# Feed-forward up product as seven block products, gated products in DRAM, and a down product with tokens stationary

## Chip, cores and metric

One core of a Trainium2 chip (trn2) runs the whole program. The metric is the device time of one execution in microseconds; the kernel before takes 2195.97 us, the median of 3 runs (2193.7 to 2197.01).

## What is computed

One inference step of a one-layer decoder over 1024 prompt tokens and 8 sample tokens (NT = 1032 columns). Attention, gated linear attention and cross attention come first and are not touched. The change is in what follows them:

```python
    u, g = jnp.split(h @ w_up, 2, axis=-1)
    g_ext = jnp.concatenate([conv_past.astype(g.dtype), g], axis=1)
    gc = conv_b + sum(conv_w[j] * g_ext[:, j:j + t] for j in range(CONV_W))
    out = (jax.nn.gelu(gc) * u) @ w_down
...
    x1 = x + merged @ p['w_o']
    ffn, conv_state = _conv_ffn(_rmsnorm(x1, p['g_ffn']), conv_past, p['w_up'], p['conv_w'], p['conv_b'], p['w_down'])
    y = x1 + ffn
```

`w_up` is 1024 x 5632 (u and g), `w_down` 2816 x 1024. The 2816 feed-forward columns are cut into 22 tiles f of 128. Everything is fp32 outside; a product is done as three fp32r matmuls, high part by high part, high by low and low by high, after each operand x is split into hi = round(x) and lo = x - hi.

## The kernel before, in words

**Merge and x1 (lines 1541 to 1578).** For each block i of 128 tokens (0 to 7, then the 8 sample tokens as block 8) the product with `w_o` runs with tokens stationary and 512 output columns moving (line 1563), 48 matmuls a block. DVE adds the result to x, SP stores the row block to `d_x1`, and `norm_rows` (ACT square, POOL power, DVE scale) gives the normed rows. One half block later `norm_turn` (line 261) turns them with 8 PE transposes and splits them by `split` (line 198: ACT writes hi, DVE writes lo) into `f_hi` and `f_lo`, 128 x 8 x 1032 each, which keep the names m_hi and m_lo in the trace.

**Up product (lines 1609 to 1644).** Per f, `dense` (line 218) is called twice, for g and for u. It loads a 128 x 8 x 128 slice of `w_up` into a `wraw` tile (three slots), splits it into `whi` and `wlo` (two slots each), and runs `mm3` (line 211) on three chunks of tokens, 384, 384 and 264 wide: 8 k by 3 = 24 matmuls a chunk, 72 a product. Chunk sums go alternately to the PSUM names bd and bt (`bank_f`). The g sums are copied by ACT into `gx_`; POOL and DVE do the convolution, ACT the gelu (lines 1627 to 1630); the u sums are multiplied on DVE and split again into `a_hi` and `a_lo`.

**Down product (lines 1602 to 1607).** After each group of three f (two in the last two groups) `down` multiplies the group's gated tiles by `w_down`, weights stationary, tokens moving, and `devac` adds each sum into `yacc`, which lies with output columns on the partitions. So at the end `y_half` (line 1673) turns `yacc` back with PE transposes, adds `x1` and stores. The last group's product and these turns are interleaved (lines 1684 to 1697).

**What sets the order.** The Tile framework takes the instructions of all engines in the order of the code as priorities and moves one forward when its inputs are there. A tile of a pool has a name and a number of slots of that name (`bufs`); a new tile waits until an older one of the same name is given back, which for a stored tile is when its DMA has landed. All the DMAs here are issued by SP, in one queue.

Of the kernel before, what the change touches and what calls it, by code (L numbers as in the profile page):

```python
# [17 lines left out]
P = 128  # L18
D = 1024
# [104 lines left out]
def body(ctx, tc, A):  # L124
# [16 lines left out]
    def bank_t():  # L141
        return pt.tile([P, 512], FT, name="bt")
# [1386 lines left out]
    with pool("fs", side="right") as fs, pool("wo") as wo:  # L1529
# [9 lines left out]
        scn = fs.tile([16, FF], FT, name="scn")  # L1539
        SY.dma_start(scn, A["state_conv"].rearrange("b t f -> (b t) f"))  # L1540
        prev = None
        mst = wo.tile([P, 8, 40], FR, name="mst")
        V.memset(mst.bitcast(FT), 0.0)
        V.tensor_copy(mst[:, :, 0:8], m_hi[:, :, S:])
        V.tensor_copy(mst[:, :, 32:40], m_lo[:, :, S:])
        for i in range(9):
            k = P if i < 8 else NB
            ts = slice(i * P, i * P + k)
            xt = wo.tile([P, D], FT, name="x2", bufs=3)
# [1 line left out]
            for hf in range(2):  # L1551
                cs = slice(hf * 512, (hf + 1) * 512)
                b = bank_s()
                if i == 8:
                    for j in range(8):
                        for w_ in range(2):
                            PE.matmul(b[:40], mst[:, j], owt[j][w_][:, cs], start=j + w_ == 0, stop=j + w_ == 8)
                    V.tensor_tensor(xt[:k, cs], xt[:k, cs], b[32:40], op=OP.add)
                else:
                    n = 0  # L1560
                    for j in range(8):
                        for a_, w_ in ((m_hi, 0), (m_lo, 0), (m_hi, 1)):
# [21 lines left out]
    sizes = (3, 3, 3, 3, 3, 3, 2, 2)
    groups = [list(range(sum(sizes[:g]), sum(sizes[:g + 1]))) for g in range(len(sizes))]
    assert groups[-1][-1] == FT_N - 1
    yacc = fp.tile([P, 8, NT], FT, name="yacc")
    GW = 2 + S + 24
    fh = lambda k: f_hi[:, k]
    fl = lambda k: f_lo[:, k]  # L1590
    ups = {}

    def devac(gi, m, c, cs, b):
        if gi == 0:
            SC.activation(yacc[:, m, cs], b, AF.Copy)
# [3 lines left out]
    def w_dn(gi):
        return A["w_down"].rearrange("(f p) m -> p f m", p=P)[:, groups[gi][0]:groups[gi][-1] + 1]  # L1600

    def down(gi):
        ats = ups.pop(gi)
        for m in range(8):
            dense(len(ats), lambda raw: SY.dma_start(raw, w_dn(gi)[:, :, m * P:(m + 1) * P]),
                  lambda k: ats[k][0], lambda k: ats[k][1],
                  lambda c, cs, b: devac(gi, m, c, cs, b), bank=bank_s)

    for gi, grp in enumerate(groups):
        ats = ups[gi] = []  # L1610
        for f in grp:
            gx_ = fp.tile([P, GW], FT, name="gx_", bufs=2)
            V.memset(gx_[:, 0:2], 0.0)
            dv = gx_[:, 2 + S:].rearrange("p (b x) -> p b x", x=3)
            V.tensor_copy(dv[:, :, 0:2], scT[:, f].rearrange("p (b t) -> p b t", t=2))

            def gevac(c, cs, b, gx_=gx_, dv=dv):
                n = b.shape[-1] - (NB if c == 2 else 0)
                SC.activation(gx_[:, 2 + cs.start:2 + cs.start + n], b[:, :n], AF.Copy)
                if c == 2:  # L1620
                    V.tensor_copy(dv[:, :, 2], b[:, n:])
            dense(8, colfill(A["w_up"], FF + f * P), fh, fl, gevac, bank=bank_f)
            V.tensor_copy(gl[f // 12][:, 0:2, f % 12], gx_[:, S:S + 2])
            V.tensor_copy(gl[f // 12][:, 2:10, f % 12], dv[:, :, 2])
            cv = fp.tile([P, GW], FT, name="cv", bufs=2)
            n = GW - 2
            G.tensor_scalar(cv[:, :n], gx_[:, :n], cwt[:, 0, f:f + 1], cwt[:, 3, f:f + 1], op0=OP.mult, op1=OP.add)
            V.scalar_tensor_tensor(cv[:, :n], gx_[:, 1:n + 1], cwt[:, 1, f:f + 1], cv[:, :n], op0=OP.mult, op1=OP.add)
            V.scalar_tensor_tensor(cv[:, :n], gx_[:, 2:n + 2], cwt[:, 2, f:f + 1], cv[:, :n], op0=OP.mult, op1=OP.add)
            SC.activation(cv[:, :n], cv[:, :n], AF.Gelu_apprx_tanh)  # L1630
            a_hi = fp.tile([P, NT], FR, name="a_hi", bufs=5)
            a_lo = fp.tile([P, NT], FR, name="a_lo", bufs=5)
            cvd = cv[:, 2 + S:2 + S + 24].rearrange("p (b x) -> p b x", x=3)[:, :, 0]

            def uevac(c, cs, b, cv=cv, cvd=cvd, a_hi=a_hi, a_lo=a_lo):
                w = b.shape[-1]
                n = w - (NB if c == 2 else 0)
                t = fp.tile([P, CW], FT, name="au", bufs=2)
                V.tensor_tensor(t[:, :n], cv[:, cs.start:cs.start + n], b[:, :n], op=OP.mult)
                if c == 2:  # L1640
                    V.tensor_tensor(t[:, n:w], cvd, b[:, n:], op=OP.mult)
                split(a_hi[:, cs], a_lo[:, cs], t[:, :w])
            dense(8, colfill(A["w_up"], f * P), fh, fl, uevac, bank=bank_f)
            ats.append((a_hi, a_lo))
            if gi and f == grp[0]:
                down(gi - 1)

    wl = []
    for k in range(2):
        raw = wp.tile([P, 1024], FT, name="wraw", bufs=3)  # L1650
        hi = wp.tile([P, 1024], FR, name="whi", bufs=2)
        lo = wp.tile([P, 1024], FR, name="wlo", bufs=2)
        SY.dma_start(raw, w_dn(gi)[:, k])
        split(hi, lo, raw)
        wl.append((hi, lo))
    x_3 = fp.tile([P, 3, D], FT, name="x_3")
    for i in range(3):
        SY.dma_start(x_3[:, i], d_x1[i * P:(i + 1) * P])
    xl = fq.tile([P, 8, NT], FR, name="m_hi").bitcast(FT)
    for i in range(3, 8):  # L1660
        SY.dma_start(xl[:, i, :D], d_x1[i * P:(i + 1) * P])
    SY.dma_start(xl[:NB, 0, :D], d_x1[S:])
    for x in range(2):
        f0, n = (0, 12) if x == 0 else (12, 10)
        b = bank_t()
        tr(b[:10 * n, :P], gl[x].rearrange("p t f -> p (t f)"))
        go_ = fp.tile([P, P], FT, name="go_", bufs=2)
        V.tensor_copy(go_[:10 * n], b[:10 * n, :P])
        for dst, r0, t in ((A["conv_p"].rearrange("b t (f p) -> (b t) f p", p=P), 0, 2),
                           (A["conv_s"][:, 1].rearrange("b (f p) -> b f p", p=P), 2 * n, 8)):  # L1670
            SY.dma_start(dst[:, f0:f0 + n], go_[r0:r0 + t * n])

    def y_half(i, hf):
        k = P if i < 8 else NB
        cs = slice(hf * 512, (hf + 1) * 512)
        xt = x_3[:, i, cs] if i < 3 else xl[:, i % 8, cs]
        b = bank_t()
        for a in range(4):
            tr(b[:k, a * P:(a + 1) * P], yacc[:, 4 * hf + a, i * P:i * P + k])
        V.tensor_tensor(xt[:k], xt[:k], b[:k], op=OP.add)  # L1680
        dst = A["y_p"].rearrange("b (i p) d -> (b i) p d", p=P)[i] if i < 8 else A["y_s"].rearrange("b t d -> (b t) d")
        SY.dma_start(dst[:, cs], xt[:k])

    for c, (c0, c1) in enumerate(CHS):
        cs = slice(c0, c1)
        for m in range(8):
            ms = slice(m * P, (m + 1) * P)
            b = bank_s()[:, :c1 - c0]
            n = 0
            for k in range(2):  # L1690
                for w_, a_ in ((0, 0), (0, 1), (1, 0)):
                    PE.matmul(b, wl[k][w_][:, ms], ats[k][a_][:, cs], start=n == 0, stop=n == 5)  # L1692
                    n += 1
            devac(gi, m, c, cs, b)
            if m % 4 == 3:
                for i in ((0, 1, 2), (3, 4, 5), (6, 7, 8))[c]:
                    y_half(i, m // 4)
# [35 lines left out]
```

## Time and profile before

| | |
|---|---|
| Median of 3 runs | 2195.97 us |
| The profiled execution's own time | 2186.02 us |
| Its span on the chip | 2184.2 us |
| PE busy | 98% of the span |
| DVE, ACT, POOL busy | 48%, 33%, 14% |
| Feed-forward part, 1420.86 us to the end | 763.3 us |

Times in rows are microseconds from the start of the span unless ns is written. PE is the matmul engine, PEld its weight load, SPq the queue that issues DMAs. A matmul row's own duration includes its passage through the pipeline; how often the next one starts is the rate.

### The profile page before, as it was taken

How to read it: one execution, taken by the hardware profiler on the slowest of the kernel's cores; microseconds unless marked ns; L12 is line 12 of the kernel's file. 1: busy time of each engine (PE TensorE's matmuls, PEld its weight loads, DVE VectorE, ACT ScalarE, POOL GpSimd, SP SyncE). 2: the span in 40 equal slices, each digit the busy share in tenths (PEclk: the TensorE clock that was granted, in tenths of full speed). 3: DMA queues.
4: the chain of work that ended last, by engine and by line, in shares of the span. 5: the costliest groups of instructions: out<-in, count | busy, mean ns of one | idle time of the engine just before them, and what ended most of it. 6: DMA issues, size and time to landing. Idle time of an engine off the chain costs nothing.

```text
span 2184.2 us, 35331 instructions
## 1 busy us (share of the span) xinstructions
PE 2138.6 (98%) x13964; PEld 1938.9 (89%) x13964; DVE 1051.5 (48%) x2618; ACT 714.8 (33%) x1545; POOL 301.2 (14%) x401
## 2 busy tenths in 40 slices
PE   7999899999999899999999999999999999999999
PEld 6999888888998798866667997799999999999998
DVE  5224455455533845288775475333243434344455
ACT  5323233333433522386653132222322121212120
POOL 3003400000100420075441310000000000000000
PEclk9999999999999999999999999999999999999999
DMA  6242633453264335631102555120211112120113
GB/s 182 97 109 85 240 110 127 174 174 117 75 213 136 102 90 147 128 89 42 39 9 90 165 165 178 68 63 26 62 36 56 51 41 59 30 67 25 59 54 129
DMA packets 241343, 213.48 MB, mean 98 GB/s; under 512 B 48614, under 2 KB 215386, under 8 KB 239626
## 3 DMA queue, kind: packets, MB, share of 16 engines
q1 hardware_dynamic: 240602, 194.45, 29.9%
q0 software_dynamic: 576, 16.78, 1.9%
q8 instruction: 110, 1.80, 0.3%
q14 instruction: 55, 0.45, 0.1%
HBM read 162.55 MB, written 48.73 MB: 97 GB/s over the span
## 4 chain that ended last, share of the span: by engine, by line
PE 86%; DMA 3%; issue 3%; DVE 2%; POOL 2%; ACT 1%; SPq 0%; POOLq 0%; ACTq 0%; DVEq 0%
PE bd L215 19%; PE bd L343 15%; PE bt L215 15%; PE bs L215 10%; PE bt L167 7%; PE bo L892 3%; PE bs L1563 3%; PE bs L765 2%; DMA Gt<-in_cache_kv,idx 2%; PE bs L591 1%; PE bd L765 1%; POOL rr L195 1%; PE bs L1692 1%; PE bs L474 1%; PE bo L1205 1%
## 5 line engine op out<-in xcount | busy, mean ns | idle before, releaser
L200 DVE TENSOR_TENSOR wlo<-wraw,whi 128x1024 fp32r<-128x1024 f32 (+3 forms) x183 | 173.0, 946 | 384.9 <-ACT whi L199 383.1
L343 PE MATMUL bd<-h_hi,whi 128*128 128x384 f32 (+1 forms) x960 | 322.1, 335 | 2.2 <-ACT st L334 2.2
L343 PE MATMUL bd<-h_lo,whi 128*128 128x384 f32 (+1 forms) x960 | 313.0, 326 | 0.0
L343 PE MATMUL bd<-h_hi,wlo 128*128 128x384 f32 (+1 forms) x960 | 312.1, 325 | 0.0
L199 ACT ACTIVATE whi<-wraw 128x1024 fp32r<-128x1024 f32 (+3 forms) x185 | 154.8, 838 | 404.1 <-PE bs L215 165.6
L343 PEld LDWEIGHTS bd<-h_hi,whi 128*128 128x128 f32 x960 | 182.0, 190 | 12.5 <-issue 8.1
L215 PE MATMUL bd<-m_lo,whi 128*128 128x384 f32 (+1 forms) x624 | 190.8, 319 | 0.0
L215 PE MATMUL bt<-m_lo,whi 128*128 128x384 f32 (+1 forms) x624 | 190.7, 319 | 0.0
L343 PEld LDWEIGHTS bd<-h_lo,whi 128*128 128x128 f32 x960 | 182.4, 190 | 3.5 <-issue 2.9
L343 PEld LDWEIGHTS bd<-h_hi,wlo 128*128 128x128 f32 x960 | 181.9, 189 | 3.1 <-issue 2.6
L215 PE MATMUL bd<-m_hi,wlo 128*128 128x384 f32 (+1 forms) x528 | 168.9, 320 | 0.0
L215 PE MATMUL bt<-m_hi,wlo 128*128 128x384 f32 (+1 forms) x528 | 168.8, 320 | 0.0
L215 PE MATMUL bd<-m_hi,whi 128*128 128x384 f32 (+1 forms) x528 | 168.7, 319 | 0.0
L215 PE MATMUL bt<-m_hi,whi 128*128 128x384 f32 (+1 forms) x528 | 168.6, 319 | 0.0
L215 PE MATMUL bs<-a_hi,wlo 128*128 128x384 f32 (+1 forms) x480 | 153.6, 320 | 0.0
L215 PE MATMUL bs<-a_lo,whi 128*128 128x384 f32 (+1 forms) x480 | 153.4, 320 | 0.0
L215 PE MATMUL bs<-a_hi,whi 128*128 128x384 f32 (+1 forms) x480 | 153.4, 320 | 0.0
L195 POOL TENSOR_TENSOR rr<-rv,cb 128x1 f32<-128x1 f32 (+7 forms) x46 | 52.3, 1138 | 649.7 <-DVE rv L194 622.5
L1597 DVE TENSOR_TENSOR yacc<-yacc,bs 128x384 f32<-128x384 f32 (+1 forms) x168 | 85.7, 512 | 89.8 <-PE bs L215 84.1
L215 PEld LDWEIGHTS bd<-m_lo,whi 128*128 128x128 f32 x624 | 115.9, 188 | 0.0
L215 PEld LDWEIGHTS bt<-m_lo,whi 128*128 128x128 f32 x624 | 115.9, 188 | 0.0
L215 PEld LDWEIGHTS bd<-m_hi,whi 128*128 128x128 f32 x528 | 99.1, 188 | 0.1
(810 smaller groups left out, 4513.3 us busy)
## 6 DMA issues: line engine op xcount, KB each, us to landing
wraw<-in_w_in SPq DMA_DIRECT2D x46, 512.0 KB
wraw<-in_w_up SPq DMA_DIRECT2D x44, 512.0 KB
tg<-d_g SPq DMA_DIRECT2D x24, 516.0 KB
d_g<-st SPq DMA_DIRECT2D x48, 192.0 KB
wraw<-in_w_down SPq DMA_DIRECT2D x48, 192.0 KB
d_z<-st SPq DMA_DIRECT2D x32, 192.0 KB
of<-d_o SPq DMA_DIRECT2D x12, 512.0 KB
xt<-in_x_prompt SPq DMA_DIRECT2D x8, 512.0 KB
```

What stands on the lines that cost most here:

```text
L167: PE.transpose(out, in_, ident[:k, :k])
L195: G.tensor_tensor(r[:k], v[:k], C("mhalf")[:k, :n], op=OP.pow)
L199: SC.activation(hi, src, AF.Copy)
L200: eng.tensor_tensor(lo, src, hi.bitcast(FT), op=OP.subtract)
L215: PE.matmul(out, a[:, k], b(k), start=n == 0, stop=n == last)
L343: PE.matmul(b, w[wi][:, k], act[:, k, t0:t1], start=k == 0 and x == 0, stop=k == 7 and x == 2)
L474: PE.matmul(mb[i], aa[:, k, i * P:(i + 1) * P], ww[:, k2 * 512:(k2 + 1) * 512], start=k == 0 and x == 0, stop=k == 7 and x == 2)
L591: PE.matmul(hv[:, 2 * s:2 * s + 2], w1[:, s, 4 * jh + j].rearrange("p r e -> p (r e)"), xT[n][:, j, :, :k], start=jh == 0 and j == 0, stop ...
L765: PE.matmul(o(bank), qt[:, x, i], kap, start=x == 0, stop=x == 1)
L892: PE.matmul(ob[kv * 64:kv * 64 + 64, :256], vS[:, br, kb, kv * 64:kv * 64 + 64], pT[:, kv], start=n == 0, stop=False)
L1563: PE.matmul(b[:k], a_[:, j, ts], owt[j][w_][:, cs], start=n == 0, stop=n == 23)
L1597: V.tensor_tensor(yacc[:, m, cs], yacc[:, m, cs], b, op=OP.add)
```

## The change

What it does, in the order of the code:

- `f_turn` takes the place of `norm_turn` in the x1 part: ACT first copies the turned block to a `wraw` tile, SP stores that to a new DRAM tensor `d_f`, and the split reads the copy. Block 8 moves from last to fifth.
- The up product of f = 0 is done as before (`plain`). For f = 1 to 21 `strassen` does both outputs, u and g, at once: the weights (u and g by two halves of the 1024 inputs) and the activations (two halves of the inputs by two halves of the 1032 tokens) are 2 x 2 blocks, and seven block products take the place of eight. Each is 4 k by 3 matmuls on two chunks of 258 tokens. Four sums of weight blocks are made per f on POOL; four sums of activation blocks are made once, by `form`, from rows of `d_f` read back into `us` tiles.
- ACT, not POOL, does the first convolution step, POOL multiplies by u, and the product goes to a new DRAM tensor `d_a`.
- After all f the down product runs by halves of the prompt tokens and halves of the 1024 outputs, with 128 tokens stationary and 512 columns of `w_down` moving, four PSUM banks in parallel. `yacc` and the turns are gone. The 8 sample tokens have a product of their own in plain fp32, in four column strips of the array.

```diff
+        def f_turn(xn, k, t0):
+            for h in range(2):
...
+                fs_ = wp.tile([P, 1024], FT, name="wraw", bufs=3)[:, :4 * k].rearrange("p (a t) -> p a t", t=k)
+                SC.activation(fs_, bv, AF.Copy)
+                SY.dma_start(d_f.rearrange("(a p) t -> p a t", p=P)[:, 4 * h:4 * h + 4, t0:t0 + k], fs_)
+                split(f_hi[:, 4 * h:4 * h + 4, t0:t0 + k], f_lo[:, 4 * h:4 * h + 4, t0:t0 + k], fs_)
...
-        for i in range(9):
+        for i in (0, 1, 2, 3, 8, 4, 5, 6, 7):
...
+    HN = NT // 2
+    QN = HN // 2
+    def zt():
+        t = fp.tile([P, 2, HN], FR, name="z", bufs=16)
...
+    def form(k):
+        fk = []
+        for r in range(2):
+            fk.append(fp.tile([P, NT], FT, name="us", bufs=2))
+            SY.dma_start(fk[r], d_f[(4 * r + k) * P:(4 * r + k + 1) * P])
+        (f11, f12), (f21, f22) = [[x[:, c] for c in cut] for x in fk]
+        t1, t2, t3, t4 = [fp.tile([P, HN], FT, name="sw", bufs=4) for _ in range(4)]
+        V.tensor_tensor(t1, f12, f11, op=OP.subtract)
+        V.tensor_tensor(t2, f22, t1, op=OP.subtract)
+        G.tensor_tensor(t3, f22, f12, op=OP.subtract)
+        G.tensor_tensor(t4, f21, t2, op=OP.subtract)
+        for n, t in ((2, t2), (3, t3), (1, t1), (4, t4)):
+            split(*tops[n][k], t)
...
+    def strassen(raw, gx_, dv, us):
+        p1, u2, u4 = [fp.tile([P, HN], FT, name=n) for n in ("p1", "u2", "u4")]
+        (a11, a12), (a21, a22) = [(r[:, :512], r[:, 512:]) for r in raw]
+        s1, s2, s3, s4 = [fp.tile([P, HN], FT, name="sw", bufs=4)[:, :512] for _ in range(4)]
+        G.tensor_tensor(s1, a21, a22, op=OP.add)
+        G.tensor_tensor(s2, s1, a11, op=OP.subtract)
...
+        X, W, Z = [[bank() for _ in range(2)] for bank in (bank_d, bank_t, bank_s)]
...
+        def product(banks, src, b, start, done):
+            w = [x.rearrange("p (k m) -> p k m", m=P) for x in w_half(src)]
+            for c in range(2):
+                n = 0
+                for k in range(4):
+                    for wi, x in ((0, 0), (0, 1), (1, 0)):
+                        PE.matmul(banks[c][:, :QN], w[wi][:, k], b[k][x][:, qs[c]], start=start and n == 0, stop=n == 11,
+                                  skip_group_check=not start)
+                        n += 1
+                done(c, banks[c][:, :QN], qs[c])
+        product(X, a11, block(0, 0), True, lambda c, b, q: SC.activation(p1[:, q], b, AF.Copy))
+        product(W, s2, tops[2], True, lambda c, b, q: V.tensor_tensor(u2[:, q], b, p1[:, q], op=OP.add))
+        product(Z, s3, tops[3], True, lambda c, b, q: None)
...
+        product(W, s1, tops[1], False, c22)
+        product(X, a12, block(1, 0), False, lambda c, b, q: SC.activation(us[:, q], b, AF.Copy))
+        product(Z, a22, tops[4], False, lambda c, b, q: V.tensor_tensor(gx_[:, 2 + c * QN:2 + (c + 1) * QN], b, u2[:, q],
+                                                                          op=OP.add))
+        product(W, s4, block(1, 1), False, lambda c, b, q: V.tensor_tensor(us[:, HN + c * QN:HN + (c + 1) * QN], b,
+                                                                             p1[:, q], op=OP.add))
+
+    def up(f):
+        raw = []
+        for c0 in (f * P, FF + f * P):
+            raw.append(wp.tile([P, 1024], FT, name="wraw", bufs=3))
+            colfill(A["w_up"], c0)(raw[-1].rearrange("p (k m) -> p k m", m=P))
+        gx_ = fp.tile([P, GW], FT, name="gx_", bufs=1)
+        us = fp.tile([P, NT], FT, name="us", bufs=2)
...
+        (plain if f == 0 else strassen)(raw, gx_, dv, us)
...
+        G.tensor_tensor(us[:, :S], cv[:, :S], us[:, :S], op=OP.mult)
+        G.tensor_tensor(us[:, S:], cvd, us[:, S:], op=OP.mult)
+        SY.dma_start(d_a[f * P:(f + 1) * P], us)
+    up(0)
+    for k in range(4):
+        form(k)
+    for f in range(1, FT_N):
+        up(f)
+    ad = fp.tile([P, FT_N, 32], FT, name="ad")
+    SY.dma_start(ad[:, :, :NB], d_a.rearrange("(f p) t -> p f t", p=P)[:, :, S:])
...
+    for half in range(2):
+        for hf in range(2):
+            banks = [bank_y() for _ in range(4)]
...
+            for f in range(FT_N):
+                rw = w_raw(nw)
+                SY.dma_start(rw, A["w_down"][f * P:(f + 1) * P, cs])
+                if hf == 0:
+                    raw = wp.tile([P, 1024], FT, name="wraw", bufs=3)
+                    SY.dma_start(raw[:, :512], d_a[f * P:(f + 1) * P, half * 512:half * 512 + 512])
+                    split(*acts[f], raw[:, :512])
+                w = w_half(rw)
+                for i in range(4):
+                    for n, (x, wi) in enumerate(((0, 0), (0, 1), (1, 0))):
+                        PE.matmul(banks[i], acts[f][x][:, i * P:(i + 1) * P], w[wi], start=f + n == 0,
+                                  stop=f == FT_N - 1 and n == 2)
+                if bdec is not None and (f % 4 == 3 or f == FT_N - 1):
+                    for j in range(f // 4 * 4, f + 1):
+                        PE.matmul(bdec[32 * (j % 4):32 * (j % 4) + 32], ad[:, j], ws[j], start=j < 4, stop=j >= FT_N - 4)
+            for i in range(4):
+                xt = ytile(i)
+                SY.dma_start(xt, d_x1[t0:t0 + P, cs])
+                V.tensor_tensor(xt, xt, banks[i], op=OP.add)
+                SY.dma_start(A["y_p"].rearrange("b t d -> (b t) d")[t0:t0 + P, cs], xt)
```

`w_half` splits a 128 x 512 block of weights into one tile of the names whi, wlo and whl in turn (two slots each). `w_raw` takes the seven slots of sw, p1, u2 and u4 in turn. P1 to P7 is what this text calls the seven calls of `product`, in their order. `C("hm")`, left out here, adds the four strips of the sample tokens' sum by one more matmul per half.

## Rows read from the trace of the kernel before

**Rows 1.** The page, parts 1 and 2: busy time; PE's clock in 40 slices.

```profile
PE 2138.6 (98%) x13964; PEld 1938.9 (89%) x13964; DVE 1051.5 (48%) x2618; ACT 714.8 (33%) x1545; POOL 301.2 (14%) x401
...
PE   7999899999999899999999999999999999999999
...
PEclk9999999999999999999999999999999999999999
```

**Rows 2.** Busy time by stretch: length, PE, PEld, DVE, ACT, POOL, clock, DMA share.

```profile
1420.86:2184.20 763.34, 758.70 (x4844) 755.66 (x4842) 316.92 (x602) 170.20 (x283) 27.37 (x23) 1.00 0.18 54
```

**Rows 3.** Chain of waits in order of time: start, length, what; matmuls per piece.

```profile
1370.67 11.10 PE bs L1563 x48
...
1512.95 34.19 PE bs L215 x216
1547.14 4.20 PE bt L215 x24
...
1555.55 2.90 PE bt L215 x24
```

**Rows 4.** PE by time, sample tokens' cross attention, fp32 in four column strips.

```profile
629.02 0.42 PE L343 MATMUL bd<-h_hi,wlo 128*128 128x384 f32 x1
629.37 0.64 PE L1237 MATMUL bo<-xkT,xqz 128*32 128x256 f32 x8
629.94 0.44 PE L343 MATMUL bd<-h_hi,whi 128*128 128x384 f32 x1
```

**Rows 5.** All engines by time, from the last prompt block of x1 on.

```profile
1411.80 0.39 PE L1563 MATMUL bs<-ol,m_hi 128*128 128x512 f32 x1
...
1416.49 1.06 PE L167 MATMUL bt<-cb,nxn 128*128 128x128 f32 x8 [0.61 <-DVE nxn L250]
...
1417.16 1.09 ACT L199 ACTIVATE m_hi<-bt 128x512 fp32r<-128x512 f32 x2 [3.01 <-PE bt L167]
```

**Rows 6.** Groups of instructions, shapes apart: POOL, ACT and DVE prices.

```profile
L558 POOL TENSOR_TENSOR qn<-qn,rr 128x512 f32<-128x512 f32 x8 | 10.7, 1332 | 0.6
...
L200 POOL TENSOR_TENSOR wlo<-wraw,whi 128x1024 fp32r<-128x1024 f32 x2 | 6.0, 2981 | 1.1 <-ACT whi L199 1.1
...
L199 ACT ACTIVATE whi<-wraw 128x512 fp32r<-128x512 f32 x24 | 15.2, 632 | 67.0 <-PE bt L215 33.8 <-PE bd L215 29.8 <-PE bd L343 3.3
...
L200 DVE TENSOR_TENSOR wlo<-wraw,whi 128x512 fp32r<-128x512 f32 x24 | 17.0, 709 | 1.8 <-ACT whi L199 0.9
```

**Rows 7.** By time, SP then ACT: a 128 KB store and 516 KB load, issue and user.

```profile
1178.10 0.36 SPq L902 DMA_DIRECT2D d_o<-ot  x1
1183.11 0.33 SPq L629 DMA_DIRECT2D of<-d_o  x1
...
1180.02 2.02 ACT L199 ACTIVATE m_lo<-of 128x1032 fp32r<-128x1032 f32 x2 [1.94 <-DMA d_o<-ot]
...
1186.96 1.07 ACT L199 ACTIVATE m_lo<-of 128x1032 fp32r<-128x1032 f32 x1 [3.62 <-DMA of<-d_o]
```

**Rows 8.** Chain of waits: a small table's load and a 512 KB weight load.

```profile
247.51 6.33 DMA pti<-in_page_table
...
735.57 3.65 DMA wraw<-in_w_in
```

**Rows 9.** The tile cwn: its load, and the transpose that reads it.

```profile
L1538 SPq DMA_DIRECT2D cwn<-in_conv_b x1: 352/352/352, 1315.7 to 1315.7; - x1
...
L167 PE MATMUL bt<-cb,cwn x1: 240/240/240, 1350.3 to 1350.3; 88*128 88x88 f32 x1
```

**Rows 10.** Busy time by stretch, after PE idled 7.35 us until 273.60.

```profile
270.00:276.00 6.00, 2.40 (x10) 2.33 (x11) 0.76 (x2) 1.79 (x4) 0.00 (x0) 0.50 0.64 236
```

**Rows 11.** ACT by time in the up product: next weights' split and last chunk's copy.

```profile
1456.39 1.06 ACT L199 ACTIVATE whi<-wraw 128x1024 fp32r<-128x1024 f32 x1 [2.34 <-PE bt L215]
1457.35 0.36 ACT L1619 ACTIVATE gx__14803<-bt 128x256 f32<-128x256 f32 x1
```

**Rows 12.** DVE by time: the last add before the last store.

```profile
2180.70 0.68 DVE L1680 TENSOR_TENSOR m_hi<-m_hi,bt 8x512 f32<-8x512 f32 x1 [0.54 <-PE bt L169]
```

More of the change, by code (lines that the diff above doesn't have):

```diff
@@ L298, in body @@
     d_x1 = dp.tile([NT, D], FT, name="d_x1")
+    d_f = dp.tile([D, NT], FT, name="d_f")
+    d_a = dp.tile([FF, NT], FT, name="d_a")
     xsrc = A["x_prompt"].rearrange("b (i p) d -> (b i) p d", p=P)
@@ L1566, in body @@
                 if hf == 0 and prev:
-                    norm_turn(*prev)
+                    f_turn(*prev)
             if i == 2:
@@ L1576, in body @@
             SY.dma_start(d_x1[ts], xt[:k])
-            prev = norm_rows(wo, xt, k, gffn), k, f_hi, f_lo, i * P
-        norm_turn(*prev)
+            prev = norm_rows(wo, xt, k, gffn), k, i * P
+        f_turn(*prev)
     mctx.close()
@@ L1582, in body @@
     fp = ctx.enter_context(pool("fp"))
[L1584 to L1587, printed above, removed]
+    HN = NT // 2
+    QN = HN // 2
     GW = 2 + S + 24
[L1589 to L1595, printed above, removed]
-        else:
-            V.tensor_tensor(yacc[:, m, cs], yacc[:, m, cs], b, op=OP.add)
@@ L1599, in w_dn @@
[L1599 to L1620, printed above, removed]
-                    V.tensor_copy(dv[:, :, 2], b[:, n:])
[L1622 to L1697, printed above, removed]
+    cut = (slice(0, HN), slice(HN, NT))
@@ new lines, in body, with block @@
+    tops = {}
+    def block(r, c):
+        return [[t[:, 4 * r + k, cut[c]] for t in (f_hi, f_lo)] for k in range(4)]
+    def zt():
+        t = fp.tile([P, 2, HN], FR, name="z", bufs=16)
+        return t[:, 0], t[:, 1]
+    def form(k):
[11 more added lines that the diff above has]
+            split(*tops[n][k], t)
@@ new lines, in body, with w_half, plain @@
+    turn3 = [0]
+    def w_half(src, eng=V):
+        turn3[0] = (turn3[0] + 1) % 3
+        if turn3[0]:
+            t = wp.tile([P, 1024], FR, name=("whi", "wlo")[turn3[0] - 1], bufs=2)
+        else:
+            t = fp.tile([P, 1024], FR, name="whl", bufs=2)
+        split(t[:, :512], t[:, 512:], src, eng)
+        return t[:, :512], t[:, 512:]
+    def plain(raw, gx_, dv, us):
+        for r, g in ((raw[1], 1), (raw[0], 0)):
+            hi = wp.tile([P, 1024], FR, name="whi", bufs=2)
+            lo = wp.tile([P, 1024], FR, name="wlo", bufs=2)
+            split(hi, lo, r)
+            w = [x.rearrange("p (k m) -> p k m", m=P) for x in (hi, lo)]
+            for c0, c1 in CHS:
+                b = bank_f()[:, :c1 - c0]
+                mm3(b, w, lambda k: f_hi[:, k, c0:c1], lambda k: f_lo[:, k, c0:c1], 8)
+                if not g:
+                    SC.activation(us[:, c0:c1], b, AF.Copy)
+                    continue
+                n = min(c1, S) - c0
+                SC.activation(gx_[:, 2 + c0:2 + c0 + n], b[:, :n], AF.Copy)
+                if c1 > S:
+                    V.tensor_copy(dv[:, :, 2], b[:, n:])
@@ new lines, in body, with bank_y, a_slot @@
+    for n in (2, 3, 1, 4):
+        tops[n] = [zt() for _ in range(4)]
+    up(0)
[4 more added lines that the diff above has]
+    ad = fp.tile([P, FT_N, 32], FT, name="ad")
+    V.memset(ad, 0.0)
+    SY.dma_start(ad[:, :, :NB], d_a.rearrange("(f p) t -> p f t", p=P)[:, :, S:])
+    am = []
+    cyc = [0]
+    def bank_y():
+        cyc[0] += 1
+        return (bank_s, bank_o, bank_d, bank_d, bank_t, bank_t, bank_s, bank_s)[cyc[0] % 8]()
+    def a_slot(n):
+        if n % FT_N >= 16 or n >= 2 * FT_N - 6:
+            if not am:
+                for name in ("m_hi", "m_lo"):
+                    t = fq.tile([P, 8, NT], FR, name=name)
+                    am.extend((t[:, i, :512], t[:, i, 512:1024]) for i in range(8))
+            return am.pop(0)
+        t = fp.tile([P, 2, HN], FR, name="z", bufs=16)
+        return t[:, 0, :512], t[:, 1, :512]
```

61 lines of the change are left out of this document (added).

## The prediction

> **What bounds the kernel now.** I read the page's busy times first: PE is busy 98% of the span, no other engine half of it, and the clock is at full speed in every slice but for idle spells [rows 1]. So time is gained by giving PE less to do, and lost where PE is made to wait. Busy time by stretch then shows the part that the change touches: from 1420.86 to the end, 763.3 us, with 758.7 of PE busy [rows 2]. There is next to no idle time to win in it. A matmul row's length says little, since matmuls overlap; the chain of waits gives the rate. 24 matmuls of 384 columns take 4.20 us and 24 of 264 take 2.90 [rows 3]. That is 175.0 and 120.8 ns each: 0.451 ns a column, and nothing to speak of beside it, though each has a weight load of its own. 48 matmuls of 512 columns take 11.10 us, 231.3 ns each [rows 3].
>
> **What is removed.** The whole 763.3 us. In it the up products are 44 x (4.20 + 4.20 + 2.90) = 497.2 us, the down product 34.2 us for each group of three f [rows 3], and the rest the last group, the turns of yacc and 4 us of tail.
>
> **Up product, f = 1 to 21.** Seven products of 4 k x 3 x 2 chunks are 168 matmuls of 258 columns. At the column price that is 120.8 - 6 x 0.451 = 118.1 ns, so 19.84 us for an f against 22.6 before, and 416.7 for 21 of them. No row has 258 columns: below, the same price a column as at 384 (117.6 ns); above, no less than the 264-wide one (120.8 ns, 9.5 us more in all). I take 118.1, since 264 is the near neighbour. f = 0 stays at 22.6 us.
>
> The TensorE page of the Trainium skill (TensorE: Matmul & The Clock Gate, section Back-to-back issue gap) gives N / 2.4 + 2.5 ns at full clock, so 162.5 ns at 384 columns and 110.0 at 258, both estimates from its formula. By it the up products would gain 52.9 us where the rows give 57.9, and the answer below would be 5 us slower; the rows, 8% above it at 384, decide.
>
> The other engines have room beside 19.84 us, by the nearest rows [rows 6]: DVE seven low parts at 0.71, ten 258-wide adds at less than that and two convolution passes at about 1.45, under 16 us; ACT seven high parts at 0.63, four copies and two wide passes, about 9; POOL four sums at 1.33 and one 1024-wide product at 2.98, about 8.7. If one of these were late at each product, the cover would be gone; that is the second rival.
>
> **Down product.** 4 passes x 22 f x 4 blocks x 3 are 1056 matmuls of 512 columns: 1056 x 231.3 ns = 244.2 us. The loads on SP (256 KB of weights and, in two passes, 256 KB of d_a for each 2.78 us) lie beside it. The sample tokens' fp32 products are new. The nearest row is four column strips of 256 columns, which hold PE from about 629.20 to 629.94, 0.74 us [rows 4]. At 512 columns a group of four costs between 0.74 and 1.48; I take 1.31, twice less the 0.17 us of entry. Ten groups of four and two of two: 10 x 1.31 + 2 x 0.74 = 14.6 us (8 to 18). The two small sums over the strips and two turns of gl: 2.2 us, by the same row. The tail stays: the last add at 2180.70 was followed by 3.5 us [rows 12], and the new end is also an add and one store; 4.0 us with the wait for PE.
>
> **Stall at the start of the part.** In x1, `f_turn` adds two ACT copies of 0.6 us [rows 6] and two SP stores a block, beside 11.1 us of matmuls [rows 3]: nothing, but for the last block. `f_turn` puts its copies into wraw slots, and the weights of f = 0 come behind them in the same three slots. Slots of a name are handed out in the order of the code. The rows agree: cwn had been issued for loading at 1315.7 and its transpose into bt ran only at 1350.3, after those of two token blocks that stand ahead of it in the code [rows 9]. It has to be so in the new code, too, or w_down loads, which wait for nothing, would take all sw slots before the first f. So g's weights of f = 0, the 20th wraw tile, wait until the 17th, block 7's first half, is stored. From the last matmul of block 7 (1412.03) to the ACT copy is 5.1 us [rows 5]; then the copy 0.6 [rows 6]; the 256 KB store about 2.5, between 1.9 for 128 KB and 3.85 for a load of 516 KB [rows 7]; the load 3.65 [rows 8]; the high part 1.06 [rows 11]; some 0.5 for the low part. That is 13.4, of which 1.0 is the block's transposes. Block 8, whose 9 us of matmuls covered this before, has moved ahead. Term: 12.5 idle and 1.0 busy (0 if a slot is free, 16 if each transfer takes 4.6).
>
> **Stall after f = 0.** The us slots are two. f = 0 has the first; `form(0)` needs two, so its second read waits until f = 0's us is multiplied and stored. From f = 0's start: product end 22.6; last copy and hand-over 0.7; POOL 2.98 and a small one 0.4 [rows 6]; store 3.9, read 3.85 [rows 7]: 34.5. Each further form costs two POOL subtractions one after the other (2 x 1.33) and a read, 6.8 with hand-overs, so the fourth's read lands at 54.9; its t2 and high part take 0.71 and 0.63 [rows 6]: 56.3. Until then PE has P1 and P5 (5.7 us) and three quarters of P2 and P3 (4.3), which wait for no fourth k. Idle: 56.3 - 22.6 - 10.0 = 23.7 us. Below: 0, if the forms run beside f = 0; above: 34, if PE finds only P1. SP's queue has nothing behind these reads that PE could use. After an idle spell of 7.35 us PE restarted at 1.2 GHz, half of its 2.4: the granted clock was 0.50 from 270 to 276, with PE at work in the last 2.4 us of that [rows 10]; I add 1.3 us for each of the two stalls, 2.6.
>
> **Stall in the first down pass.** ad waits for f = 21's store. Its product leaves POOL some 6 us after PE's last up matmul, the store lands 3.9 later, ad's 2816 pieces take perhaps 6.33 (the small table's load, [rows 8]): at 16 us. The seven w_down slots then free up, and the eighth tile's load and split (4.2) end at 21.5 with the group, where PE wants them at 7 x 2.78 = 19.5. Term 3 us (0 to 10).
>
> **Sum.** 12.5 + 1.0 + 22.6 + 23.7 + 2.6 + 416.7 + 244.2 + 14.6 + 2.2 + 3 + 4.0 = 747.1 us in place of 763.3: 16.2 us less. The profiled execution took 2186.02, so it would come to 2169.8; the median of the runs stands 10 us above that execution, and I take the difference over: 2195.97 - 16.2 = 2180 us. So PE's work falls by 55 us, and two thirds of that are spent again on waits that come once each.
>
> **Rivals.**
> - *The waits are hidden.* If the planner lets the forms run beside f = 0, the 23.7 and 1.3 us go: 2155 us. For it: f = 0 is left in the old form, which leaves 22.6 us of cover. Against it: the slots, two for nine tiles in a row. Chance 0.18.
> - *The convolution delays the next f on DVE (slower than before).* At each change of f, DVE has two convolution passes of 1.45 us in its queue. If P2's low part stands behind them and P1's 2.84 us are not enough cover, PE waits. From 0.77 us per f (16.2 / 21) the gain is gone; at 1.5 us it is 31 us and the time 2211. Against it: ACT took the next weights' split ahead of the last chunk's copy [rows 11], so work that is ready does move forward, and the weights have six half slots. Chance 0.14.
> - *258 columns are not cheaper.* If the narrow matmul has a floor near 122.7 ns, 4.6 ns on 3528 matmuls take back the 16.2 us: 2196, no change. Against it: 264 and 384 lie on one line [rows 3]. With the upper ends of the stalls, which give the same, 0.13.
> - *My forecast.* Chance 0.55; its own range is 2166 to 2191.
>
> **How the numbers follow.** About 0.2%, 4.4 us, is what a measurement of this kernel can tell from no change. Faster by more than that are my forecast and the first rival, 0.73; within it 0.13; slower 0.14. The range reaches down to near the first rival, which the bounds of the first stall could carry past (2155), and up to 2198, where the upper ends of both stalls (4 and 10 us) and of the down pass (7) meet the sum; it leaves out most of the second rival.
>
> **What would show it.** In the new trace: P1 to P7 at 2.83 us each in the chain and 19.8 us from f to f; PE idle some 12 us ahead of its first up matmul, released by the split of a wraw load that follows a store to d_f; some 24 us idle after f = 0, in pieces that end with forms; the down passes at 2.78 us an f. I am wrong if an f takes over 20.6 us, if the forms' reads come before f = 0's store, or if the fp32 strips take 3 us a group.

## Result and profile after

The changed kernel takes 2211.64 us, the median of 4 runs (2210.39 to 2213.78), beside 2195.05 us of the kernel before on the same chip (4 runs): ratio 1.0076, 95% interval 1.0058 to 1.0093. It is slower by 16.6 us where I had forecast 16 us faster.

The page of the changed kernel, parts 1 and 2 (busy time; PE and its clock in 40 slices), answers to [rows 1]:

```profile
PE 2103.7 (95%) x13952; PEld 1840.2 (83%) x13952; DVE 1127.8 (51%) x2710; ACT 818.8 (37%) x1716; POOL 477.5 (22%) x515
...
PE   7999899999999899999999999955999999999999
...
PEclk9999999999999999999999999977999999999999
```

PE is busy 35 us less, and yet the span is longer. Two slices give it away: PE half busy, its clock at 0.7.

The two profiled spans differ by 24.1 us, more than the medians. By the end of attention, where nothing is changed, the new execution is 7.9 us behind already (the x1 matmul that waits for `oh`, PE by time, before and after). What the change adds from there on is 16.2 us (24.1 less 7.9), near the 16.6 us between the medians. So times of two runs are set against each other from that matmul on.

```profile
1327.83 0.50 PE L1563 MATMUL bs<-oh,m_hi 128*128 128x512 f32 x1 [1.70 <-ACT oh L199]
```

```profile
1335.76 0.50 PE L1575 MATMUL bs<-oh,m_hi 128*128 128x512 f32 x1 [2.02 <-ACT oh L199]
```

Busy time by stretch, from that matmul on (columns as in [rows 2]): x1; the start stall; f = 0; P1 and the second stall; the block products; the down product:

```profile
1335.76:1430.55 94.79, 94.26 (x448) 74.24 (x448) 35.42 (x54) 24.73 (x48) 4.39 (x8) 0.98 0.36 116
1430.55:1445.24 14.69, 1.94 (x8) 1.57 (x9) 4.27 (x9) 4.59 (x8) 0.55 (x1) 0.58 0.60 170
1445.24:1470.22 24.98, 24.98 (x144) 24.54 (x145) 6.71 (x11) 7.40 (x10) 0.00 (x0) 0.91 0.23 69
1470.22:1510.85 40.63, 3.03 (x27) 2.83 (x25) 22.13 (x24) 12.11 (x21) 20.24 (x13) 0.59 0.34 104
1510.85:1935.50 424.65, 422.63 (x3505) 422.20 (x3506) 262.80 (x510) 169.31 (x280) 181.24 (x122) 0.99 0.27 84
1935.50:2208.30 272.80, 263.87 (x1152) 199.91 (x1150) 96.94 (x144) 76.24 (x123) 3.37 (x2) 0.99 0.46 146
```

PE by time shows what it waited for (in brackets the idle time before the row and what ended it):

```profile
1434.79 1.94 PE L167 MATMUL bt<-cb,nxn 128*128 128x128 f32 x8 [4.25 <-DVE nxn L250]
1445.24 0.69 PE L215 MATMUL bt<-m_hi,whi 128*128 128x384 f32 x1 [8.51 <-ACT whi L199]
1510.85 1.23 PE L1668 MATMUL bt<-z,wlo 128*128 128x258 f32 x4 [37.60 <-ACT wlo L199]
1514.09 4.47 PE L1668 MATMUL bt<-z,wlo 128*128 128x258 f32 x20 [2.02 <-DVE wlo L200]
1951.70 1.08 PE L1779 MATMUL bt<-sw,ad 128*32 128x512 f32 x4 [4.88 <-DMA ad<-d_a]
```

These five idle spells are 57 us: 12.75 before f = 0, 39.6 after it (37.60 and, inside P2, 2.02), 4.9 in the first down pass. The long one is read in the chain of waits (start, length, what):

```profile
1473.50 2.64 DMA d_a<-us
1476.16 3.34 DMA us<-d_f
...
1479.75 1.68 POOL sw L1618
1481.42 1.70 POOL sw L1619
1483.14 4.31 DMA us<-d_f
...
1491.08 4.45 DMA us<-d_f
...
1499.17 4.01 DMA us<-d_f
...
1514.09 4.47 PE bt L1668 x20
```

The store of f = 0's gated product gives back a `us` slot; then four times a read of `d_f` and two POOL differences, 7.0 us for the first turn and 8.0 for each further one (1483.14 to 1491.08); then the weights of P2. That last part is seen in POOL by time, then DVE by time, and in one row of ACT by time:

```profile
1503.34 1.76 POOL L1618 TENSOR_TENSOR sw<-us 128x516 f32<-128x516 f32 x1 [4.20 <-DMA us<-d_f]
1505.06 1.73 POOL L1619 TENSOR_TENSOR sw<-us,sw 128x516 f32<-128x516 f32 x1
1506.87 1.59 POOL L1655 TENSOR_TENSOR sw<-wraw 128x512 f32<-128x512 f32 x1
1508.54 1.59 POOL L1656 TENSOR_TENSOR sw<-sw,wraw 128x512 f32<-128x512 f32 x1
...
1520.31 1.29 POOL L1655 TENSOR_TENSOR sw<-wraw 128x512 f32<-128x512 f32 x1 [6.82 <-DMA wraw<-in_w_up]
```

```profile
1510.61 1.75 DVE L200 TENSOR_TENSOR whi<-sw,whi 128x512 fp32r<-128x512 f32 x1
1512.29 1.75 DVE L200 TENSOR_TENSOR wlo<-sw,wlo 128x512 fp32r<-128x512 f32 x1
1513.96 0.68 DVE L200 TENSOR_TENSOR whl<-sw,whl 128x512 fp32r<-128x512 f32 x1
1514.56 0.68 DVE L200 TENSOR_TENSOR wlo<-wraw,wlo 128x512 fp32r<-128x512 f32 x1
```

```profile
1512.38 0.61 ACT L199 ACTIVATE wlo<-wraw 128x512 fp32r<-128x512 f32 x1
```

f = 1's weights were in SBUF long before, but their sums s1 and s2 (lines 1655, 1656) stand behind the last form in POOL's queue, and the splits behind the forms' splits in DVE's. The ACT row is the split of P5's weights, which needs no sum and yet stands behind the splits of the sums. After that there is no idle time until the down product: the first P5 starts at 1524.16 us and the last at 1926.68, 20 f later, 20.13 us each. The chain has the single products:

```profile
1532.95 2.87 PE bd L1668 x24
1535.81 2.90 PE bt L1668 x24
```

### The profile page after: what moved, and what is told of

Read it like the earlier page. It is cut to its first block, busy times and chain, and to the rows that moved or that the text cites. A ratio compares the mean times of both kernels' runs of the same rounds, so it can differ in the third digit from the quotient of the medians.

```text
span 2208.3 us, 36252 instructions
## 1 busy us (share of the span) xinstructions
PE 2103.7 (95%) x13952; PEld 1840.2 (83%) x13952; DVE 1127.8 (51%) x2710; ACT 818.8 (37%) x1716; POOL 477.5 (22%) x515
## 4 chain that ended last, share of the span: by engine, by line
PE 59%; issue 5%; DMA 3%; DVE 2%; POOL 1%; ACT 1%; SPq 0%; POOLq 0%; DVEq 0%; ACTq 0%
PE bt L1668 8%; PE bd L345 6%; PE bs L1668 5%; PE bd L1668 5%; PE bt L167 5%; PE bd L1775 4%; PE bs L1575 4%; PE bo L894 3%; PE bt L215 3%; PE bd L215 3%; PE bs L1775 3%; PE bs L767 2%; PE bo L1775 2%; PE bt L1775 2%; PE bd L767 1%
## 5 line engine op out<-in xcount | busy, mean ns | idle before, releaser
L345 PE MATMUL bd<-h_hi,whi 128*128 128x384 f32 (+1 forms) x960 | 323.3, 337 | 2.9 <-ACT st L336 2.9
L345 PE MATMUL bd<-h_lo,whi 128*128 128x384 f32 (+1 forms) x960 | 314.6, 328 | 0.0
L345 PE MATMUL bd<-h_hi,wlo 128*128 128x384 f32 (+1 forms) x960 | 313.7, 327 | 0.0
L199 ACT ACTIVATE whi<-wraw 128x1024 fp32r<-128x1024 f32 (+1 forms) x106 | 92.9, 877 | 202.0 <-PE bd L345 58.3
L200 DVE TENSOR_TENSOR wlo<-wraw,whi 128x1024 fp32r<-128x1024 f32 (+1 forms) x83 | 89.1, 1076 | 136.8 <-ACT whi L199 135.6
L894 PE MATMUL bo<-pT,vS 128*64 128x256 f32 x528 | 86.1, 405 | 0.1
L215 PE MATMUL bd<-h_hi,whi 128*128 128x384 f32 (+1 forms) x264 | 85.3, 324 | 0.0
L215 PE MATMUL bd<-h_lo,whi 128*128 128x384 f32 (+1 forms) x264 | 85.0, 322 | 0.0
L215 PE MATMUL bd<-h_hi,wlo 128*128 128x384 f32 (+1 forms) x264 | 84.6, 320 | 0.0
L1668 PE MATMUL bt<-z,wlo 128*128 128x258 f32 x336 | 45.1, 292 | 39.6 <-ACT wlo L199 37.6
L781 POOL TENSOR_SCALAR s_s<-s_s,rs,gates 128x128 f32<-128x128 f32 (+7 forms) x64 | 54.6, 853 | 125.6 <-DVE rs L851 105.3
L1668 PEld LDWEIGHTS bt<-z,wlo 128*128 128x128 f32 x336 | 43.4, 199 | 40.1 <-ACT wlo L199 37.8
L1711 POOL TENSOR_TENSOR us<-cv,us 128x1024 f32<-128x1024 f32 x22 | 61.9, 2815 | 68.5 <-ACT us L1644 37.6
```

The lines of the kernel that those rows point to most:

```text
L199: SC.activation(hi, src, AF.Copy)
L200: eng.tensor_tensor(lo, src, hi.bitcast(FT), op=OP.subtract)
L215: PE.matmul(out, a[:, k], b(k), start=n == 0, stop=n == last)
L345: PE.matmul(b, w[wi][:, k], act[:, k, t0:t1], start=k == 0 and x == 0, stop=k == 7 and x == 2)
L781: G.tensor_scalar(t, t, rs[:, i, br:br + 1], gv[:, i // 2, i % 2, br:br + 1], op0=OP.mult, op1=OP.mult)
L894: PE.matmul(ob[kv * 64:kv * 64 + 64, :256], vS[:, br, kb, kv * 64:kv * 64 + 64], pT[:, kv], start=n == 0, stop=False)
```

## The experiments

All times are ratios to the kernel before on the same chip; "by ratio" means (ratio - 1) x 2195 us. The changed kernel is +16.7 by ratio.

### Own tiles for what the forms read

```diff
-            fk.append(fp.tile([P, NT], FT, name="us", bufs=2))
-            SY.dma_start(fk[r], d_f[...])
+            SY.dma_start(fk[r], d_f[...])   # fk: the z tiles that the form fills afterwards
```

> The forms read f into the tiles that they fill afterwards, not into the two us slots; nothing else changes. Theory A (slots: the 39.6 us idle after f = 0 is a loop of two us slots, 2.6 us for f = 0's store to land, then four turns of a load of 3.3 to 4.5 us and 3.4 us of POOL): the reads go out during f = 0, the forms run beside it, the idle falls to 0 to 8 us, time about 2176 us (2172 to 2182). Rival B (the arithmetic: POOL keeps the forms behind f = 0's own product and its four turns of 3.45 us, with f = 1's weight sums behind them, stay): idle about 20 us, 2192 us. Rival C (something else holds P2, the weights of f = 1 for example): idle over 33 us, over 2205 us.

Ratio 0.9959 (0.9944 to 0.9974): 9 us faster than before and 26 faster than the changed kernel. The idle time after f = 0 is 9.9 us in place of 39.6, in three pieces (PE by time):

```profile
1476.34 0.39 PE L1670 MATMUL bd<-m_hi,whi 128*128 128x258 f32 x1 [3.88 <-ACT us L1646]
...
1480.78 1.23 PE L1670 MATMUL bt<-z,wlo 128*128 128x258 f32 x4 [2.18 <-ACT wlo L199]
...
1485.87 0.58 PE L1670 MATMUL bs<-z,whl 128*128 128x258 f32 x1 [3.86 <-ACT whl L199]
```

Theory A has the larger part: 30 us of the stall were the two slots. Its 2176 us were too few (2186 by ratio), since 9.9 us idle stay where I had allowed 8 at most and set the time by 4; that is 6 of the 10 us, and the rest lies within the two intervals. What stays ends with ACT's copy of f = 0's u and with the splits of f = 1's weight sums, which is rival B's arithmetic.

### The last block's copies out of the weight slots

```diff
+            st = wo.tile([P, D], FT, name="x2", bufs=3) if t0 == 7 * P else None
-                fs_ = wp.tile([P, 1024], FT, name="wraw", bufs=3)
+                fs_ = wp.tile([P, 1024], FT, name="wraw", bufs=3) if st is None else st[:, 512 * h:]
```

> The copies of the last token block on their way to d_f stand in a tile of the x1 phase, not in the weight slots. Theory (f = 0's gate weights wait for the slot of a stored copy): they are there before x1 ends, f = 0 starts on tokens of the earlier blocks while the last block's norm runs, the 12.75 us idle before f = 0 nearly goes, and with it some us at half clock: about 2197 us (2195 to 2200). Rival (the norm and the turns of the last block, 4.24 us idle, stand ahead of f = 0 in TensorE's queue): only the 8.5 us piece goes, 2203 us. Rival (a slot further back, or SP's queue, holds the weights): 2211 us.

Ratio 1.0033 (1.0021 to 1.0044), 2202 us by ratio, 9.5 less than the changed kernel. That is the first rival's time, but PE by time shows the theory's way:

```profile
1431.67 0.69 PE L215 MATMUL bd<-m_hi,whi 128*128 128x384 f32 x1 [2.90 <-ACT whi L199]
1433.01 1.94 PE L167 MATMUL bt<-cb,nxn 128*128 128x128 f32 x8 [0.34 <-DVE nxn L250]
1499.34 1.23 PE L1669 MATMUL bt<-z,wlo 128*128 128x258 f32 x4 [37.91 <-ACT wlo L199]
```

f = 0 now starts ahead of the last block's turns, on tokens of earlier blocks. 3.2 us are idle in place of 12.75, and the difference is the gain: the slot was the cause. The theory's 14 us had the 2.9 us that stay in it, and some half clock, but PE still restarts at half speed: the granted clock was 0.50 from 1431.67 to 1437.00. The second stall is as long as ever.

### Both

> Both edits: own tiles for the forms' reads, and the last block's copies out of the weight slots. If the two stalls are separate, the gains add: 2211.6 less about 36 and about 14, 2162 us (2155 to 2170). Rival: with f = 0 starting 12 us sooner, the forms' reads of d_f have 12 us less to come in before P2 wants them, so that the idle moves there: 2172 to 2178 us.

Ratio 0.9951 (0.9933 to 0.9969), 2184 us by ratio and 2 better than own tiles alone: the rival, and by more than it said. The start stall is 3.6 us, but 20.3 us are idle after f = 0 (the two pieces below and 2.02 us inside P2). SP by time and PE by time:

```profile
1437.35 3.66 SPq L1616 DMA_DIRECT2D z<-d_f  x6
1463.61 0.32 SPq L1716 DMA_DIRECT2D d_a<-us  x1
1463.97 1.26 SPq L1616 DMA_DIRECT2D z<-d_f  x2
```

```profile
1460.12 0.39 PE L1671 MATMUL bd<-m_hi,whi 128*128 128x258 f32 x1 [2.74 <-ACT us L1647]
1477.40 1.23 PE L1671 MATMUL bt<-z,wlo 128*128 128x258 f32 x4 [15.59 <-ACT wlo L199]
```

Counted from the x1 matmul that waits for `oh` (1333.49 here, 1337.64 with own tiles alone), f = 0 starts 12.6 us sooner (1429.70 against 1446.42), and yet P2 starts 0.8 us later (1477.40 against 1480.78): the forms end when they end. And the last two reads stand behind the store of f = 0's product in SP's queue.

### Reads first

```diff
+        if f == 0:
+            for k in range(4):
+                read(k)      # both reads of form(k), ahead of f = 0's products
```

> As e3, with all eight reads of f issued ahead of f = 0's products, so that the last two don't stand in SP's queue behind f = 0's gated store (in e3 they left at 1464 us, the first six by 1441). Theory (the reads were the last thing in e3): idle after f = 0 falls from 20.3 to under 8 us, 2168 us. Rival (the arithmetic: in e3 POOL had only 2.65 us of wait for that read, and its fourth turn, f = 1's two weight sums of 3.3 us and VectorE's splits stand behind it anyway): 17 us idle, 2178 us.

Ratio 0.9916 (0.9900 to 0.9933). All eight reads leave from 1438.45 us on, and 16.8 us are still idle, 3.6 less than in the run before: the rival. The ratio fell by more than that (0.35%, 8 us), with intervals that touch; I don't explain the rest. The reads were no longer what the forms waited for.

### The forms on DVE alone

```diff
-        G.tensor_tensor(t3, f22, f12, op=OP.subtract)
-        G.tensor_tensor(t4, f21, t2, op=OP.subtract)
+        V.tensor_tensor(t3, f22, f12, op=OP.subtract)
+        V.tensor_tensor(t4, f21, t2, op=OP.subtract)
```

> As e5, with the two of a form's four differences that POOL computed on VectorE as well. Theory (POOL is the queue: a difference takes it 1.6 to 1.8 us against 0.69 on VectorE, and while POOL runs VectorE takes 1.7 us in place of 0.69): a form costs VectorE 8 x 0.69 = 5.5 us, four 22 us, POOL has only the product and f = 1's weight sums, which are ready early: idle 5 to 10 us, 2170 us. Rival (VectorE is the queue already, with the convolution of f = 0 in it): idle as in e5 or longer, 2178 to 2185 us.

Ratio 0.9907 (0.9888 to 0.9926), by itself not to be told from the run before; but the idle time in the profile is 12.7 us, 4 us less, with eight operations more on the engine that looked busier. DVE by time, then POOL and PE:

```profile
1464.91 0.69 DVE L1623 TENSOR_TENSOR sw<-z 128x516 f32<-128x516 f32 x1
1465.52 0.68 DVE L1624 TENSOR_TENSOR sw<-z,sw 128x516 f32<-128x516 f32 x1
1466.12 4.63 DVE L200 TENSOR_TENSOR z<-sw,z 128x516 fp32r<-128x516 f32 x4
1470.68 1.75 DVE L200 TENSOR_TENSOR whi<-sw,whi 128x512 fp32r<-128x512 f32 x1
```

```profile
1466.89 1.65 POOL L1660 TENSOR_TENSOR sw<-wraw 128x512 f32<-128x512 f32 x1 [1.84 <-DVE z L200]
```

```profile
1470.92 1.23 PE L1673 MATMUL bt<-z,wlo 128*128 128x258 f32 x4 [11.29 <-ACT wlo L199]
```

Differences that POOL had done in 1.7 us take DVE 0.69, and it takes 1.75 for one of its own again as soon as POOL is at f = 1's weight sums (1470.68). The theory has the direction; the idle time is longer than its 5 to 10 us, since DVE is on the path to the end. And f = 1's weight sums are not ready early, as it had them, though POOL is free of the forms: the first (L1660) waits for a DVE split of the last form, at 1466.89. The forms' differences and the weight sums share the four slots of `sw`, so a sum has to wait until a difference is split. No run gave the sums slots of their own.

### No trip to DRAM

```diff
-            SY.dma_start(fk[r], d_f[...])
+            (G if t is f21 else V).tensor_tensor(t, hi, lo, op=OP.add)   # for f11, f12, f21, f22
```

> No d_f: the forms sum f's high and low parts again from SBUF (three of the four sums of a form on VectorE, one on POOL), and the last turn splits straight from PSUM as before the change. Theory: no store, no read, the forms begin with the last block's turn at about 1434 us and cost VectorE 9 x 0.7 = 6.2 us and POOL 3 x 1.7 = 5.1 us each, slowed beside each other to 7 or 8: done 30 us later, about 1465, against P2 wanted at 1457: idle 8 to 12 us, 2170 us. Rival (VectorE and POOL slow each other as in the stall itself, 1.7 us an operation): 9 x 1.2 x 4 = 43 us, idle 20 us or more, 2180 us or more.

Ratio 0.9927 (0.9909 to 0.9944), 21.8 us idle after f = 0: the rival. The stretch from the last turn to P2 in one row (columns as above):

```profile
1430.00:1475.00 45.00, 23.20 (x156) 22.54 (x154) 42.67 (x48) 18.17 (x31) 27.73 (x16) 0.80 0.03 12
```

DVE is busy for 42.67 of 45 us. Without store or read P2 starts no sooner than with the reads first: 143.8 us after the x1 matmul that waits for `oh` (1474.87 less 1331.08), there 141.8 (1475.16 less 1333.40). The four sums a form that take the trip's place fill DVE; what the trip by itself costs, this run can't show.

### Two plain f

```diff
-        (plain if f == 0 else strassen)(raw, gx_, dv, us)
+        (plain if f < 2 else strassen)(raw, gx_, dv, us)
```

> As e3, with f = 1 by plain products too, so that the forms have 22.6 us more to finish in. Theory (the forms are late, and nothing else is wrong with them): no idle over 2 us after f = 0, f = 1 costs 22.6 in place of 20.1 us, 2181 less 20 less about 2 of half clock plus 2.5: 2162 us. Rival (the wait goes along, to the weights of the first block products, which POOL sums behind the forms): idle 5 to 15 us, 2167 to 2177 us.

On top of both edits: ratio 0.9922 (0.9896 to 0.9949), idle 9.1 us: the rival's size. PE waits for ACT's copies of f = 1's u. Ahead of the first of them in ACT's queue stand the last form's splits and then those of f = 2's weight sums, which POOL makes behind the forms, so it is the rival's cause by a detour (PE by time, then ACT):

```profile
1483.96 0.58 PE L1671 MATMUL bd<-m_hi,whi 128*128 128x258 f32 x1 [6.51 <-ACT us L1647]
1489.44 0.39 PE L1671 MATMUL bd<-m_hi,whi 128*128 128x258 f32 x1 [2.54 <-ACT us L1647]
```

```profile
1479.45 0.63 ACT L199 ACTIVATE wlo<-sw 128x512 fp32r<-128x512 f32 x1 [2.55 <-POOL sw L1659]
...
1483.43 0.47 ACT L1647 ACTIVATE us<-bd 128x384 f32<-128x384 f32 x1
```

### Forms behind f = 1, and ad in two

```diff
     up(0)
+    up(1)                      # plain
     for k in range(4):
         form(k)
```

> As e9 with f = 1 by plain products too, and the forms written behind f = 1, so that they rank behind its copies and its convolution in every queue. Theory (forms with 22.6 us more cover, on VectorE and ACT alone, with no copy of TensorE's banks behind them): idle after f = 0 under 3 us, time e9's 2172 less 10 of idle, less 1 of half clock, plus 2.5: 2164 us, ratio 0.987. Rival (as in e7, TensorE waits for ACT, whose 16 splits stand ahead of a copy): 5 to 9 us idle, 2169 us, ratio 0.989.

With the reads first and the forms on DVE: ratio 0.9865 (0.9849 to 0.9880), 2165 us by ratio. One wait of 2.17 us is left after f = 0 and 1, and the granted clock from 1426 to 1480 us is 0.97 (0.81 with the forms on DVE and one plain f). Theory and size are right. Against the run with the forms on DVE two things differ, the plain f and the order, and no run parts them.

> As e11, with the sample tokens' gated products read in two parts (f 0 to 15, f 16 to 21), so that the first strip doesn't wait for the last f's store. Theory: the 5 us idle in the first down pass (4.9 in the changed kernel, 7.7 in e7) goes, nothing else moves: 5 us under e11. Rival (the last f's own rows are wanted for the pass itself some us later, so the wait only goes there): the same time as e11 within 2 us.

Ratio 0.9867 (0.9849 to 0.9884): not to be told from the run before. The first strip's wait in the profile (7.58 us there) is gone, and 2.02 us turn up for the last f's own split:

```profile
1904.90 1.94 PE L1788 MATMUL bt<-sw,ad 128*32 128x512 f32 x8 [7.58 <-DMA ad<-d_a]
```

```profile
1901.08 0.50 PE L1786 MATMUL bo<-whi,z 128*128 128x512 f32 x1 [2.02 <-ACT whi L199]
```

Theory (5 us) and rival (within 2) both fit the spread of its four runs, so this edit's worth stays open.

### All plain, and the down half alone

```diff
-        (plain if f == 0 else strassen)(raw, gx_, dv, us)
+        plain(raw, gx_, dv, us)
```

> All 22 f by plain products as f = 0, with no forms and no block products; the down product and the start stall stay. Theory (a plain f costs 22.6 us and seven block products 20.1, and the change pays for its 21 times 2.5 us with 39.6 us idle): 2211.6 less 39.6, less about 3 us of half clock, plus 52: 2221 us (2216 to 2226), f to f 22.6. Rival (plain products run into waits of their own, of gx_ and cv with one slot each): over 2230 us. Rival (a block product f saves under 2 us): under 2212 us.

Ratio 1.0099 (1.0080 to 1.0118), +22 us by ratio, 5 more than the changed kernel. 22.62 us from f to f and no waits between them, as the theory has it; its 2221 us (2217 by ratio) left out that plain products don't run into ad's wait (4.9). With the rows: 21 f at 2.49 us saved are 52 us, against 39.6 idle, 3.0 of half clock behind it, and 4.9 for ad. What is left is 5.

> Only the down half of the change: all f by plain products, no forms and no d_f (turns split straight from PSUM), gated products through DRAM, down product with tokens stationary. Theory (the down half is worth nothing: from the traces, before spends 763.3 us from the end of x1, of which 22 x 22.62 are up; the new down passes took 272.8 us with the sample tokens' wait of 4.9, which plain products don't show): the time of before within 4 us, ratio 1.000 (0.998 to 1.002). Rival (the turns that it removes were worth their columns, about 10 us): ratio 0.995. Rival (the strips in plain fp32 and the DRAM trip cost 10 us): 1.005.

The same with `norm_turn` in place of `f_turn`. Ratio 1.0021 (1.0010 to 1.0032), 4.6 us slower than before. The theory's range reaches to 1.002, but its point, 1.000, lies outside the interval, the rivals' 0.995 and 1.005 as well: the down half costs a little. Between this run and the one above lies what `f_turn` costs: 0.78%, 17 us. In the trace of all plain that is 13.0 us idle, 1.9 for the turns that nothing covers any more, and 2.4 us of half clock in f = 0.

## Why the prediction was wrong

Its sum against the stretches above, in us, from x1 on:

| Term | predicted | measured |
|---|---|---|
| x1 to its last matmul, against before | 0 | +1.8 |
| start stall | 12.5 + 1.0 | 12.75 + 1.94 |
| f = 0 | 22.6 | 25.0 |
| stall after f = 0 | 23.7 | 39.6 |
| f = 1 to 21, with the clock | 416.7 + 2.6 | 425.7 |
| down product, strips, ad, tail | 268.0 | 272.8 |

The differences are 32.5 us, which is the miss of -16.2 against +16.2. Most of the +1.8 of x1 isn't the change's: own tiles and all plain, with the same x1, take 93.3 us for it, the changed kernel 94.8.

**The step that failed is the stall after f = 0**, by 15.9 us; everything else together would have left a forecast of no change. Its first half was right: the second read behind the store of f = 0's product, predicted to have landed 34.5 us after f = 0's start, landed at 34.3 (1479.5). That is in part luck: f = 0 ended 2.4 us late, and POOL's product (2.6 against 3.4), the store (2.64 against 3.9) and the read (3.34 against 3.85) made up for it. Three things after that were wrong.
- A further form takes 8.0 us, not 6.8: POOL's difference takes 1.7 us, not the 1.33 of [rows 6], with DVE at work beside it, and the reads 4.3 in place of 3.85. In all 3.0 us.
- "Until then PE has P1 and P5 (5.7 us) and three quarters of P2 and P3 (4.3)": it had P1, 3.0 of 10.0 us. P2's first matmul wants its weights, and these come from POOL behind all four forms. I had counted POOL's sums as beside the work and not asked what they queue behind. P5 ran only behind P2 to P4 (1524.16), and its own weights were split only at 1512.38. In all 7.0 us.
- After the fourth form's read came POOL's two differences, two weight sums and the splits, 9.7 us with the 2.02 inside P2, where the sum had 1.4 for one difference and its high part: 8.3 us, for the same reason.

Less 2.4 us, by which f = 0 ended late, these are the 15.9. The experiments bear out the cause as far as the slots go (own tiles: 30 us less idle) and that the two engines are next (forms on DVE: 4 us less, no trip: DVE full). How the 9.7 us fall into parts is read from the trace alone, and with the forms on DVE the weight sums still came late, by the slots of `sw`; no run moved the sums by themselves. They also show that the rival "the waits are hidden" was not to be had by freeing the slots alone.

**The rest of the sum.** The start stall was right in place and size, and its cause was shown by the run that moved the last copies. The clock cost 2.4 us in f = 0 and 3.0 after the second stall, against 2.6 (the granted clock was 1.00 in P1 and 0.50 from 1510.85 to 1515.00). A block product's matmul takes 20.13 / 168 = 119.8 ns, against 118.1 and within its bounds: 6.0 us more over 21 f. The formula of the Trainium skill (TensorE: Matmul & The Clock Gate, section Back-to-back issue gap), which the page gives for a single matmul by itself, comes to an estimate of 110.0 ns at 258 columns. The measured 119.8 ns is further from it than from the column price of [rows 3]. The down passes have 2.79 us an f where no strip stands, 1.0 us more in all; the wait for ad took 4.9 in place of 3, and strips and small sums about 1.9 more, part of it at half clock behind that wait (granted clock 0.61 from 1951.70 to 1956.00). The tail was right. That the down half is slower than what it replaced I had as 268.0 against 266.1 (763.3 less 497.2), without saying so; the run with the down half alone has 4.6 us. The upper end of the range was also added up wrong: 2180 with 4, 10 and 7 us more is 2201, not 2198. The measured time lies above both.

**The rivals.** The second rival names 2211 us, which is the measured time, but by accident: the convolution delays nothing, for between 1514 us and the down product PE has no wait. 258 columns have no floor at 122.7: they take 119.8.

## What to carry to other kernels

A change that adds a one-time preparation is priced by its queues and its slots: for every engine that prepares, and every slot name it uses, write down what the first consumer needs and what stands ahead of it, weights and copies too, and not only the data under preparation. Two stalls that lie one behind the other don't add up when removed; the second was measured from a start that the first had pushed back. Here 52 us of saved matmuls went for the most part into slot names used for two purposes (`wraw`, `us`, and `sw` behind them). From the changed kernel to the best one lie 46 us by ratio, 0.9865 of the kernel before in place of 1.0076. Own tiles and the moved copies brought back 27 of them; reads first, the forms on DVE, and one more f done the old way with the preparation written behind it brought the rest, the last step 9.

## What was unexpected of the hardware

DVE and POOL slowed each other here where both worked on SBUF tensors. Beside POOL, DVE's 512-wide difference starts every 1.68 us; as soon as POOL stops, every 0.6 (1510.61, 1512.29, 1513.96, 1514.56). POOL's sum takes 1.29 us alone (1520.31) and 1.59 beside DVE (1506.87, 1508.54), its differences 1.73 to 1.76. The prediction used both engines' prices alone. The Trainium skill has the rule (SBUF — State Buffer, section SBUF: two separate sides): a DVE operation with two SBUF inputs and a POOL operation that reads SBUF share a port pair that the first to start holds for the whole instruction, while the other waits. The trace agrees in what it does to the time; it does not show the lock itself.
